# A gated hybrid-attention layer on one core: x enters the products without its norm, which is multiplied onto the products' columns

## The chip, the cores and the metric

The kernel runs on one core of one Trainium2 chip. The metric is the device time of one execution in microseconds (us); the time of a kernel is the median of several executions.

## The reference

One layer on x of 512 tokens (S) by 2048 features (D), everything in float32:

```
h    = x * rsqrt(mean(x*x) + eps) * norm_g
proj = h @ w_in                      # 3 branches x (q, k, v, gate) x 512, 4 forget logits, 3 x 2048 merge-gate logits
A: softmax attention with forget gates, q and k normalised per head     (4 heads of 128)
B: chunked attention with a relative bias, q and k normalised per head  (4 heads)
C: stick-breaking attention, q and k plain                              (4 heads)
y    = branch output * silu(gate);  up = y @ w_up (per branch)
out  = x + (sum over branches of sigmoid(merge gate) * up) @ w_out
```

The factor rsqrt(mean(x*x)+eps), called rstd below, is one number per token. norm_g is one number per feature.

## The kernel before, in words

All matrices are held transposed: a tile has 128 features on its partitions and the 512 tokens along its row. x is 16 such tiles, the k tiles (kt 0 to 15). A product of 128 output columns of w_in (a "column" below) with all of x is 16 k tiles of matmuls.

**Precision.** Each float32 operand is split in two fp32r parts: hi is a rounded copy made by ScalarE (L243), lo is the rest, made by VectorE (L247). A product takes hi*hi, hi*lo and lo*hi: three matmuls of 512 for each k tile. Weights come from HBM as raw tiles of 128x1024 (8 k tiles) and are split in the same way into `wh` and `wl`. There are three `wh` and three `wl` buffers, so the split runs two units ahead of TensorE (`LA = 2`). A unit is one weight tile with its matmuls.

**Two kinds of product.** A plain column (`col_task`, L554) is two units, 48 matmuls of 512. A `PairTask` (L603) makes two columns by a Strassen-like scheme over token halves and feature halves: seven units, each with 8 matmuls of 512 (one weight part times hi and lo of a half) and 8 of 256. It needs combinations of the raw weights (VectorE, L646 and L652, and one DMA that adds, issued by POOL in L278), combinations of x (`combos`, L506), and it folds its accumulators with VectorE and ScalarE (`after_of`, L697). The first pair is of a "late" form, which needs the combinations of x later.

**Order of the units.** `first_quad` (L1252) makes q, k, v and gate of head (C,0) at once, k tile after k tile as x arrives, and the forget logits: nine units, with kt 0, then 1, then two k tiles for each unit. Then come four plain merge-gate columns (`first_head`, L1333), the late pair, and eleven heads, each with a pair for q and k, a pair of merge gates, a pair for v and gate, and another pair of merge gates; head (C,1) has only one pair of merge gates. The attention of a head is cut into stages that are started at given units (`OFF`, L1640). Then `up_units` (L1420) and `out_pair` (L1540) follow.

**The norm.** Each k tile of x is multiplied by norm_g (`prep_x`, L426: VectorE L433 for kt below 10, ScalarE L436 above) and split; `first_quad` uses that unnormalised x. At the same time x is loaded a second time in natural layout (`xn`), squared and summed (L466), and `norm_x` (L460) makes rstd, spread over all partitions by one matmul (L481). `split_n` (L495) multiplies all 16 tiles by rstd (L501) and splits them again in place, and every later product uses the normalised x. The four columns of `first_quad` are multiplied by rstd when they are taken from PSUM (L1289), the forget logits too (L1300).

**What sets the order of instructions.** TensorE, ScalarE and VectorE run in a fixed order that a small planner (`Flow`, L63) writes down when the kernel is built: each task yields (engine, cost, due time), and on each engine the ready task with the earliest due time goes next. On the chip each engine takes its list strictly in order. SP issues nearly all loads and stores, POOL the adding DMAs. Work tiles of 128x512 come from a pool `t2` of 21 buffers (`NT`); raw weights have six.

Of the kernel before, what the change touches and what calls it, by code (L numbers as in the profile page):

```python
# [161 lines left out]
def hybrid_kernel(  # L162
# [126 lines left out]
    nc.scalar.dma_start(small_in, consts)  # L289
# [118 lines left out]
    norm_ev = [Event() for _ in range(KT)]  # L408
    used_q = [Event() for _ in range(KT)]
    used_g = [Event() for _ in range(UK)]  # L410
    x1 = [Parts("x1", [norm_ev[k], Event()]) for k in range(UK)]
    x2 = [Parts("x2", [norm_ev[k + UK]] * 2) for k in range(UK)]
# [6 lines left out]
    xps.free.clear()  # L419


    xnat = [xp.tile([P, 2, S], F32, tag="x", name=nm("xn")) for _ in range(UK)]
# [3 lines left out]
    def prep_x(kt):  # L426

        due = (5.0 + 3.2 * kt,)
        yield x_in[kt]
        x = xraw[kt]  # L430
        if kt < 10:
            yield (DVE, 0.5, *due)
            nc.vector.tensor_scalar_mul(x, x, gn[:, kt:kt + 1])  # L433
# [22 lines left out]

    rstd, rstd_ev = [], Event()
    n_split = [0]

    def norm_x():  # L460

        for i in range(NQ * QB):
            yield n_in[i]
            yield ACT, 0.75, 12.0 + 1.5 * i
            x = xnat[i // 2][:, i % 2, :]
            nc.scalar.activation(x, x, AF.Square, accum_out=ssq[:, i // NQ, i % NQ:i % NQ + 1])  # L466
        give(xps, UK)
        small_n = cp.tile([P, 5, QB], F32, name="small_n")
        y, m, tmp = small_n[:, 0, :], small_n[:, 1, :], [small_n[:, i, :] for i in range(2, 5)]
        yield DVE, 0.2  # L470
        nc.vector.tensor_reduce(m, ssq, axis=AX.X, op=ALU.add)
        yield from rsqrt(y, m, D, tmp, 4)
        yield t2s, 1
        dg = t2("dg")
        for b in range(QB):
            yield ACT, 0.3
            nc.scalar.activation(dg[:, blk(b)], identf, AF.Copy, scale=y[:, b:b + 1])
        yield atts, 1
        ps = att()
        yield PE, 0.9  # L480
        nc.tensor.matmul(ps, onef, dg, start=True, stop=True)  # L481
# [8 lines left out]
    def rstd_used():  # L490
        n_split[0] += 1
        if n_split[0] == KT + 5:
            give(t2s)

    def split_n(kt):  # L495

        due = (52.0 + 1.0 * kt + (8 if kt >= UK else 0),)
        yield raw_ev[kt]
        yield rstd_ev
        yield (DVE, dve_us(S), *due)  # L500
        nc.vector.tensor_mul(xraw[kt], xraw[kt], rstd[0])  # L501
        yield used_q[kt]
        yield from split(xs[kt].hi, xs[kt].lo, two(xraw[kt]), S, norm_ev[kt], due)
        rstd_used()

    def combos(k):  # L506

        due = (96.0 + k,)
        late = (106.0 + k,)
        a, b = xraw[k], xraw[k + UK]  # L510
        yield norm_ev[k]
        yield norm_ev[k + UK]
# [9 lines left out]
        yield used_g[k]  # L522
# [30 lines left out]

    def col_task(srcs, evac, bank=0, used=None):  # L554

        st = {}

        def mms(i):
            def go(u):
                if i == 0:  # L560
                    yield accs[bank], 1
                    st["ps"] = acc(bank)
                ps = two(st["ps"])
                for j in range(UK):
                    kt = i * UK + j
                    yield norm_ev[kt]
                    yield PE, mm_us(S, 2)
                    mm(ps, u.hi[:, j, :], xs[kt].hi, kt == 0)
                    mm(ps, u.hi[:, j, :], xs[kt].lo)
                yield u.ready  # L570
                for j in range(UK):
                    kt = i * UK + j
                    yield PE, mm_us(S)
                    mm(ps, u.lo[:, j, :], xs[kt].hi, stop=kt == KT - 1)
                    if used is not None and i == 0:
                        set_(used[j])
            return go

        def after():
            yield from evac(st["ps"])  # L580
            give(accs[bank])
        return [Unit(mms(i), after if i == 1 else None, srcs=[srcs[i]]) for i in range(2)]
# [336 lines left out]
    class Head:  # L919
# [53 lines left out]
        def plain(self, r):  # L973
            yield self.event(r)
            yield from self.turn()
            c = self.c[r]
# [111 lines left out]
        def stick_scores(self, j):  # L1088
            n = S - j * P
            for e in (("p", Q), ("p", K)):  # L1090
                yield self.event(*e)
            yield from self.room_of("z", j, 1)
# [9 lines left out]
            nc.scalar.activation(z, ps, AF.Copy, scale=SCALE)  # L1102
# [46 lines left out]
        def v_trans(self):  # L1149
# [10 lines left out]
            self.v = pair_of("v")  # L1160
            yield from split(*self.v, ps, S, self.event("v"))
            give(atts)

        def silu(self):

            yield self.event(G)
            g = self.c[G]
            yield t2s, 1
# [71 lines left out]
    def gate_units(late=False, x1_first=False):  # L1240
        n, d = gates.pop(0)

        def keep(i):
            def go(c):
                spill(n, d + i, c)
                return
                yield
            return go
        units.extend(PairTask(gate_col(n, d), gate_col(n, d + 1), ops, keep(0), None, keep(1), late,
                              x1_first=x1_first).units)  # L1250

    def first_quad(head):  # L1252

        c0 = head.n * 4 * NH + head.h
        ps = {}

        spans = [(0, 1), (1, 2)] + [(k, k + 2) for k in range(2, KT, 2)]

        def mms(i):
            def go(u):  # L1260
                if i == 0:
                    for r in (Q, K, V, G):
                        pool = atts if r in (V, G) else accs[0]
                        yield pool, 1
                        ps[r] = att() if r in (V, G) else acc()
# [18 lines left out]
        def take(r):  # L1284
            def go():
                yield t2s, 1
                yield DVE, dve_us(S)
                c = t2("c")
                nc.vector.tensor_mul(c, ps[r], rstd[0])  # L1289
                give(atts if r in (V, G) else accs[0])  # L1290
                rstd_used()
                head.c[r] = c
                set_(head.event(r))
            return go

        def take_f():
            yield t2s, 1
            yield DVE, dve_us(S)
            v = t2("f")[:2 * NH, :]
            nc.vector.tensor_mul(v, first_ps[:2 * NH, :], rstd[0][:2 * NH, :])  # L1300
            give(atts)
            rstd_used()
# [4 lines left out]
        def after():  # L1307
            for r in (Q, K, V, G):
                spawn(take(r)(), 1.0, flow.fin)
# [10 lines left out]
    def spilled(n, d):  # L1320
        def evac(ps):
            yield t2s, 1
            yield ACT, act_us(S)
            c = t2("c")
            nc.scalar.activation(c, ps, AF.Copy)
            spill(n, d, c)
        return evac

# [20 lines left out]
    def head(n, h, last=False):  # L1349
# [3 lines left out]
        if not last and (n, h) != (C, 1):  # L1353
# [3 lines left out]
        if last:  # L1357
            gate_units(x1_first=True)
# [225 lines left out]
    def loads():  # L1584
# [5 lines left out]
        def n(i):  # L1590
            n_in[i].t = fetch(xnat[i // 2][:, i % 2, :], xn[i // NQ, i % NQ], 0.0, 256).t

        order = [("x", 0), ("w", 0), ("x", 1), ("w", 1), ("x", 2), ("x", 3), ("w", 2)] + [("n", i) for i in range(6)]
        order += [("x", 4), ("x", 5), ("w", 3)] + [("n", i) for i in range(6, 12)] + [("x", 6), ("x", 7), ("w", 4)]
        order += [("n", i) for i in range(12, 16)] + [("x", 8), ("x", 9), ("w", 5)]
        order += [("x", i) for i in range(10, KT)]
        for kind, i in order:
            if kind == "x":
                yield from x(i)
            elif kind == "n":  # L1600
                n(i)
            else:
                yield from load_unit(units[i])
        for u in units[6:]:
# [20 lines left out]
    spawn(norm_x(), 5.0)  # L1625
    for kt in range(KT):
        spawn(split_n(kt), 5.0)
# [55 lines left out]
```

## Time and profile before

| what | value |
|---|---|
| time, median of 3 (lowest to highest) | 1346.86 us (1345.76 to 1347.42) |
| the profiled execution's own time | 1347.36 us |
| its span, first to last instruction | 1345.6 us |
| matmuls | 7514 |
| HBM read, written | 241.03 MB, 19.69 MB |

The profile is one execution. A page gives busy time by engine, a row of 40 slices of the span, a chain followed back from the last instruction, and groups of instructions. PE is TensorE's matmul queue, PEld its weight loads, DVE VectorE, ACT ScalarE. A row of a timeline is: start in us, how long, engine, line and operation, out<-in, shape, count, and in brackets the idle time ahead of it with what ended it. A matmul's shown time reaches beyond the start of the next one, since matmuls overlap; the step from start to start is what it costs.

### The profile page before, as it was taken

How to read it: one execution, taken by the hardware profiler on the slowest of the kernel's cores; microseconds unless marked ns; L12 is line 12 of the kernel's file. 1: busy time of each engine (PE TensorE's matmuls, PEld its weight loads, DVE VectorE, ACT ScalarE, POOL GpSimd, SP SyncE). 2: the span in 40 equal slices, each digit the busy share in tenths (PEclk: the TensorE clock that was granted, in tenths of full speed). 3: DMA queues.
4: the chain of work that ended last, by engine and by line, in shares of the span. 5: the costliest groups of instructions: out<-in, count | busy, mean ns of one | idle time of the engine just before them, and what ended most of it. 6: DMA issues, size and time to landing. Idle time of an engine off the chain costs nothing.

```text
span 1345.6 us, 20021 instructions
## 1 busy us (share of the span) xinstructions
PE 1333.1 (99%) x7514; PEld 1161.3 (86%) x7514; DVE 1098.2 (82%) x1585; ACT 801.3 (60%) x1240; POOL 94.2 (7%) x125
## 2 busy tenths in 40 slices
PE   7999999999999999999999999999999999999999
PEld 5789888888888888888888888888888888898888
DVE  5898997978878797787978878788788877797786
ACT  6656665656565666656666656656567655454543
POOL 0000000000001000010010101000000000000100
PEclk9999999999999999999999999999999999999999
DMA  9556666677677776776776777777767855658883
GB/s 305 197 145 170 161 169 191 164 211 190 179 193 200 193 191 191 192 198 194 188 200 183 187 195 178 191 189 201 180 173 222 288 201 189 200 148 246 252 243 102
DMA packets 91585, 262.03 MB, mean 195 GB/s; under 512 B 10184, under 2 KB 16968, under 8 KB 91488
## 3 DMA queue, kind: packets, MB, share of 16 engines
q1 hardware_dynamic: 72384, 201.69, 44.6%
q0 software_dynamic: 14976, 54.53, 24.5%
q10 hardware_dynamic: 4128, 4.53, 1.0%
q8 instruction: 59, 0.97, 0.3%
q14 instruction: 38, 0.31, 0.1%
HBM read 241.03 MB, written 19.69 MB: 194 GB/s over the span
## 4 chain that ended last, share of the span: by engine, by line
PE 95%; DMA 2%; DVE 1%; SPq 1%; issue 0%; ACT 0%; ACTq 0%; DVEq 0%
PE acc L262 82%; PE att L262 7%; DMA xn<-in_xn 1%; PE att L1130 1%; PE att L1059 1%; DMA raw<-in_w_col 1%; PE att L1197 1%; PE att L1198 1%; PE att L258 1%; PE att L259 1%; PE att L257 1%; PE att L1196 1%; DVE wl L247 1%; SPq L274 1%; PE att L1157 0%; DVE m L247 0%
## 5 line engine op out<-in xcount | busy, mean ns | idle before, releaser
L247 DVE TENSOR_TENSOR wl<-raw,wh 128x1024 fp32r<-128x1024 f32 (+2 forms) x413 | 493.8, 1196 | 161.9 <-ACT wh L243 161.4
L243 ACT ACTIVATE wh<-raw 128x1024 fp32r<-128x1024 f32 (+2 forms) x413 | 427.4, 1036 | 139.0 <-PE acc L262 59.8
L262 PE MATMUL acc<-x,wh 128*128 128x512 f32 (+1 forms) x1632 | 417.8, 391 | 7.4 <-ACT wh L243 7.4
L262 PEld LDWEIGHTS acc<-x,wh 128*128 128x128 f32 x1632 | 288.2, 189 | 58.1 <-ACT wh L243 8.1
L262 PE MATMUL acc<-t,wh 128*128 128x512 f32 (+1 forms) x1080 | 274.1, 390 | 0.0
L262 PEld LDWEIGHTS acc<-x,wl 128*128 128x128 f32 x1504 | 210.5, 190 | 19.0 <-DVE x L433 0.3
L262 PE MATMUL acc<-x,wl 128*128 128x256 f32 (+1 forms) x1504 | 223.6, 289 | 0.0
L262 PEld LDWEIGHTS acc<-t,wh 128*128 128x128 f32 x1080 | 189.5, 189 | 30.7
L262 PEld LDWEIGHTS acc<-t,wl 128*128 128x128 f32 x1056 | 144.8, 190 | 10.9
L262 PE MATMUL acc<-t,wl 128*128 128x256 f32 x1056 | 148.4, 282 | 0.0
L278 POOL DMA_DIRECT2D raw<-in_w_col x88 | 76.1, 865 | 939.2 <-DMA raw<-in_w_col 499.1
L262 PE MATMUL acc<-m,wh 128*128 128x512 f32 (+1 forms) x512 | 114.1, 366 | 0.3 <-DVE m L247 0.2
L262 PEld LDWEIGHTS acc<-m,wh 128*128 128x128 f32 x512 | 85.4, 189 | 13.6 <-DVE m L247 1.1
L830 ACT ACTIVATE c<-acc 128x256 f32<-128x256 f32 x49 | 18.8, 383 | 91.7 <-PE acc L262 88.7
L797 ACT ACTIVATE u<-acc 128x512 f32<-128x512 f32 x49 | 29.2, 596 | 73.1 <-PE acc L262 73.1
L262 PE MATMUL att<-y,wh 128*128 128x512 f32 x256 | 65.8, 389 | 0.0
L262 PEld LDWEIGHTS acc<-m,wl 128*128 128x128 f32 x448 | 60.5, 190 | 4.6 <-DVE wl L247 0.9
L646 DVE TENSOR_TENSOR raw<-raw,raw 128x1024 f32<-128x1024 f32 x52 | 63.4, 1219 | 0.5
L652 DVE TENSOR_TENSOR raw<-raw,raw 128x1024 f32<-128x1024 f32 x52 | 63.4, 1218 | 0.4
L262 PE MATMUL acc<-m,wl 128*128 128x256 f32 x448 | 62.6, 283 | 0.5 <-DVE wl L247 0.5
L780 ACT ACTIVATE v<-acc 128x512 f32<-128x512 f32 x50 | 29.9, 598 | 46.6 <-PE acc L262 46.6
L262 PEld LDWEIGHTS att<-y,wh 128*128 128x128 f32 x256 | 48.1, 188 | 9.9
(216 smaller groups left out, 1402.0 us busy)
## 6 DMA issues: line engine op xcount, KB each, us to landing
raw<-in_w_col SPq DMA_DIRECT2D x235, 512.0 KB, 4.4
raw<-in_w_col POOLq DMA_DIRECT2D x88, 512.0 KB, 6.4
raw<-in_w_out SPq DMA_DIRECT2D x40, 512.0 KB, 4.4
gl<-c SPq DMA_DIRECT2D x48, 256.0 KB, 2.4
raw<-in_w_up SPq DMA_DIRECT2D x32, 384.0 KB, 3.1
sg<-gl SPq DMA_DIRECT2D x48, 256.0 KB, 4.6
raw<-in_w_out POOLq DMA_DIRECT2D x16, 512.0 KB, 6.7
xn<-in_xn SPq DMA_DIRECT2D x16, 256.0 KB, 7.3
```

What stands on the lines that cost most here:

```text
L243: nc.scalar.activation(hi, src, AF.Copy)
L247: nc.vector.tensor_sub(lo, src, f(hi))
L257: nc.tensor.matmul(ps, lh, rh, start=start, stop=False, skip_group_check=more)
L258: nc.tensor.matmul(ps, lh, rl, start=False, stop=False, skip_group_check=more)
L259: nc.tensor.matmul(ps, ll, rh, start=False, stop=stop, skip_group_check=more)
L262: nc.tensor.matmul(ps, w, x, start=start, stop=stop, skip_group_check=more)
L278: nc.gpsimd.dma_start(to, src, accum_op=ALU.add)
L646: nc.vector.tensor_add(w[1], w[1], w[5])
L652: nc.vector.tensor_add(w[2], w[2], w[1])
L780: nc.scalar.activation(self.v, ps, AF.Copy)
L797: nc.scalar.activation(self.s, ps, AF.Copy)
L830: nc.scalar.activation(c, ps[:, RH], AF.Copy, scale=-1.0)
```

## The change

- `prep_x` splits x times norm_g straight from the loaded tile: ScalarE copies with the scale norm_g, VectorE computes x*norm_g - hi in one instruction. The tile itself is multiplied by norm_g later (kt even VectorE, odd ScalarE), for `combos`. x is never multiplied by rstd; `split_n` is gone.
- Every column that needs the norm is multiplied by the spread rstd when it is finished (`by_norm`): the 48 merge-gate columns, q and k of A and B, q of C, all gate columns, the forget logits. For C the keys' factor goes into the scale of the scores, and for all heads v gets it per token after its transposition, in four pieces of 128.
- The four plain merge-gate columns and `col_task` are gone. Their two pairs are made as pairs: one in head (C,1), one in the last head.
- `first_quad` takes its k tiles in the order 0, 1, 8-9, 2-3, 10-11, 4-5, 12-13, 6-7, 14-15, and q and k use other PSUM banks. Its columns are copied from PSUM without rstd.
- The loads: the second copy of x (`xn`) is loaded after the sixth unit's weights, three tiles for each unit, into `t2` buffers. The constants (norm_g among them) are loaded through POOL's queue instead of ScalarE's.
- `combos` is due earlier, and the stages of the first head start at other units.

The core of the diff:

```diff
-    nc.scalar.dma_start(small_in, consts)
+    nc.gpsimd.dma_start(small_in, consts)
...
     def prep_x(kt):
...
-        x = xraw[kt]
-        if kt < 10:
+        x, g, h, lo = xraw[kt], gn[:, kt:kt + 1], xs[kt].hi, xs[kt].lo
+        yield (ACT, act_us(S), *due)
+        nc.scalar.activation(h, two(x), AF.Copy, scale=g)
+        set_(raw_hi[kt])
+        yield (DVE, dve_us(S), *due)
+        nc.vector.scalar_tensor_tensor(lo, two(x), g, f(h), op0=ALU.mult, op1=ALU.subtract)
+        set_(raw_ev[kt])
+
+        due = (DUE[0] - 16.0 + place[kt],)
+        if kt % 2 == 0:
             yield (DVE, 0.5, *due)
-            nc.vector.tensor_scalar_mul(x, x, gn[:, kt:kt + 1])
+            nc.vector.tensor_scalar_mul(x, x, g)
         else:
             yield (ACT, 0.65, *due)
-            nc.scalar.activation(x, x, AF.Copy, scale=gn[:, kt:kt + 1])
-        yield from split(xs[kt].hi, xs[kt].lo, two(x), S, raw_ev[kt], due, raw_hi[kt])
+            nc.scalar.activation(x, x, AF.Copy, scale=g)
+        set_(gained[kt])
...
+    def by_norm(c, src=None):
+
+        yield rstd_ev
+        yield DVE, dve_us(S)
+        nc.vector.tensor_mul(c, c if src is None else src, rstd[0][:c.shape[0], :])
+        n_used[0] += 1
+        if n_used[0] == NB * DT + NB * NH + NH + 4 * NH + 1:
             give(t2s)
 
-    def split_n(kt):
-
-        due = (52.0 + 1.0 * kt + (8 if kt >= UK else 0),)
-        yield raw_ev[kt]
-        yield rstd_ev
-        yield (DVE, dve_us(S), *due)
-        nc.vector.tensor_mul(xraw[kt], xraw[kt], rstd[0])
-        yield used_q[kt]
-        yield from split(xs[kt].hi, xs[kt].lo, two(xraw[kt]), S, norm_ev[kt], due)
-        rstd_used()
...
         def keep(i):
             def go(c):
+                yield from by_norm(c)
                 spill(n, d + i, c)
...
-            yield from split(*self.v, ps, S, self.event("v"))
+            self.v = h, lo = pair_of("v")
+            yield rstd_ev
+            yield ACT, 4 * act_us(P)
+            for b in range(QB):
+                nc.scalar.activation(h[:, blk(b)], ps[:, blk(b)], AF.Copy, scale=rcol[:, b:b + 1])
+            yield DVE, 4 * dve_us(P)
+            for b in range(QB):
+                nc.vector.scalar_tensor_tensor(lo[:, blk(b)], ps[:, blk(b)], rcol[:, b:b + 1], f(h[:, blk(b)]),
+                                               op0=ALU.mult, op1=ALU.subtract)
...
-        cols = []
-        for _ in range(2):
-            g, d = gates.pop(0)
-            cols += [(g, d), (g, d + 1)]
-        t = [col_task(gate_col(*c), spilled(*c), b, used_g if i == 3 else None)
-             for i, (c, b) in enumerate(zip(cols, (1, 2, 0, 0)))]
-        for i in range(2):
-            units.extend(u[i] for u in t)
...
-        if not last and (n, h) != (C, 1):
+        if not last:
             gate_units()
...
         if last:
+            gate_units()
             gate_units(x1_first=True)
...
-OFF = dict(cs=3, ct=12, s=11, t=17, v=1, av=8, s1=8, t1=13, v1=0, av1=3, fb=31, a0=18, b0=28)
+OFF = dict(cs=3, ct=12, s=11, t=17, v=1, av=8, s1=8, t1=13, v1=0, av1=3, fb=24, a0=11, b0=20)
+
+DUE = 48.0, 58.0
+N_FROM, N_PER = 5, 3
```

More of the change, by code (lines that the diff above doesn't have):

```diff
@@ L418, in hybrid_kernel @@
     atts.free.pop()
-    xps.free.clear()
-    xnat = [xp.tile([P, 2, S], F32, tag="x", name=nm("xn")) for _ in range(UK)]
+    del xps.free[UK:]
+    spans = [(0, 1), (1, 2)] + [(k + h, k + h + 2) for k in range(0, UK, 2) for h in (0, UK)][1:]
+    place = {kt: i for i, kt in enumerate(kt for sp in spans for kt in range(*sp))}
     n_in = [Event() for _ in range(NQ * QB)]
@@ L552, in halves @@
         return [w_col[c, 0], w_col[c, 1]]
[L554 to L582, printed above, removed]
     class Pair(Unit):
@@ L974, in plain @@
             yield self.event(r)
+            c = self.c[r]
+            if r == Q:
+                yield from by_norm(c)
             yield from self.turn()
[L976 removed]
             yield t2s, 2
@@ L1167, in silu @@
             g = self.c[G]
+            yield from by_norm(g)
             yield t2s, 1
@@ L1284, in take @@
         def take(r):
-            def go():
-                yield t2s, 1
-                yield DVE, dve_us(S)
[L1288 to L1294, printed above, removed]
+            yield t2s, 1
+            c = t2("c")
+            if r in (Q, V):
+                yield ACT, act_us(S)
+                nc.scalar.activation(c, ps[r], AF.Copy)
+            else:
+                yield DVE, dve_us(S)
+                nc.vector.tensor_copy(c, ps[r])
+            give(pools[r])
+            head.c[r] = c
+            set_(head.event(r))
         def take_f():
+            yield rstd_ev
             yield t2s, 1
-            yield DVE, dve_us(S)
             v = t2("f")[:2 * NH, :]
-            nc.vector.tensor_mul(v, first_ps[:2 * NH, :], rstd[0][:2 * NH, :])
+            yield from by_norm(v, first_ps[:2 * NH, :])
             give(atts)
-            rstd_used()
             nc.sync.dma_start(fd, v)
@@ L1590, in n @@
         def n(i):
[L1591 to L1604, printed above, removed]
+            yield t2s, 1
+            t = t2("xn")
+            n_in[i].t = fetch(t, xn[i // NQ, i % NQ], 0.0, 256).t
+            spawn(square_x(i, t), 10.0)
+        todo = list(range(NQ * QB))
+        for i, sp in enumerate(spans):
+            for kt in [kt for sp in spans[i:i + 2 if i else 1] for kt in range(*sp)]:
+                if xraw[kt] is None:
+                    yield from x(kt)
+            yield from load_unit(units[i])
+            if i >= N_FROM:
+                for _ in range(N_PER):
+                    if todo:
+                        yield from n(todo.pop(0))
+        for i in todo:
+            yield from n(i)
+        for u in units[len(spans):]:
             yield from load_unit(u)
```

79 lines of the change are left out of this document (34 added, 45 removed).

## The prediction

> **What bounds the kernel now.** I read the page first, then what TensorE waited for, then the windows, then the timeline of the first 70 us.
>
> ```profile
> span 1345.6 us, 20021 instructions
> PE 1333.1 (99%) x7514; PEld 1161.3 (86%) x7514; DVE 1098.2 (82%) x1585; ACT 801.3 (60%) x1240; POOL 94.2 (7%) x125
> PE 95%; DMA 2%; DVE 1%; SPq 1%; issue 0%; ACT 0%; ACTq 0%; DVEq 0%
> ...
> PE acc L262 <- ACT wh L243: 7.4, 2, 7.0
> PE att L481 <- ACT dg L477: 1.2, 1, 1.2
> PE acc L262 <- DVE wl L247: 0.5, 1, 0.5
> PE acc L262 <- DVE m L247: 0.2, 1, 0.2
> ```
>
> TensorE is the bound. It is busy in 99% of the span, it is 95% of the chain that ended last, and it waited 9.3 us in all, of which 7.0 is its first start. So only two things can shorten the kernel by more than a few us: fewer matmul steps, or less standing still in the first stage.
>
> ```profile
> 0.00:20.00 20.00, 13.04 (x48) 9.57 (x49) 10.30 (x25) 10.25 (x22) 2.79 (x18) 1.00 0.86 292
> 20.00:40.00 20.00, 18.34 (x79) 13.09 (x77) 10.20 (x17) 16.67 (x41) 0.00 (x0) 1.00 1.01 333
> 40.00:60.00 20.00, 20.00 (x88) 15.01 (x87) 19.13 (x28) 14.85 (x23) 0.00 (x0) 1.00 0.56 194
> 60.00:80.00 20.00, 20.00 (x90) 16.33 (x89) 19.69 (x36) 8.05 (x11) 1.01 (x1) 1.00 0.52 130
> 120.00:1050.00 930.00, 930.00 (x5440) 820.41 (x5440) 767.54 (x1079) 582.97 (x898) 74.88 (x88) 1.00 0.72 190
> ```
>
> The columns are PE, PEld, DVE, ACT, POOL busy, then the granted clock, the DMA share and GB/s. In the first 40 us TensorE has holes while the DMA engines are full (share 0.86 and 1.01). From 40 us on it has none, and the clock is 1.00. From 120 to 1050 us VectorE works 767.5 of 930 us (83%) without holding TensorE up.
>
> **Part 1: two merge-gate pairs in place of four plain columns.**
>
> ```profile
> 63.61 3.79 PE L262 MATMUL acc<-x,wh 128*128 128x512 f32 x16
> 67.23 1.98 PE L262 MATMUL acc<-x,wl 128*128 128x512 f32 x8
> 69.05 3.79 PE L262 MATMUL acc<-x,wh 128*128 128x512 f32 x16
> ...
> 202.28 19.57 PE acc L262 x112
> ```
>
> A plain unit has 16 + 8 matmuls and takes 69.05 - 63.61 = 5.44 us. Four columns are eight units: 43.5 us. The last row is a stretch of seven pair units in the chain, 7 x (8 of 512 + 8 of 256) = 112 matmuls: 19.57 us for two columns. Two pairs take 39.1 us. TensorE is the bound at both places, so the gain is whole: **-4.4 us**. No other matmul is added or dropped; the attention has the same ones.
>
> **Part 2: the first stage.** The change takes 16 x 256 KB of `xn` out from between the first weights.
>
> ```profile
> 27.86 0.61 PE L262 MATMUL att<-x,wl 128*128 128x512 f32 x2
> 28.88 0.73 PE L262 MATMUL acc<-x,wh 128*128 128x512 f32 x2 [0.41 <-ACT wh L243]
> ...
> 37.65 0.40 PE L262 MATMUL att<-x,w 128*8 128x512 f32 x1
> 39.30 1.10 PE L481 MATMUL att<-dg,tmpc 128*128 128x512 f32 x2 [1.25 <-ACT dg L477]
> ```
>
> With 0.23 us from matmul to matmul, the two matmuls from 27.86 should be followed at 28.32, not 28.88: 0.56 us lost, to a weight split that waited for its DMA. The one at 37.65 should be followed at 37.88, not 39.30: 1.42 us lost, to the matmul that spreads rstd. Together 2.0 us. After the change a unit of 28 matmuls (some 6.5 us) needs 1 MB of x and weights, 160 GB/s, where the windows show 290 to 330: the first hole goes (-0.56). The matmul that spreads rstd stays, and in the changed kernel's order it comes after the sixth unit of `first_quad`'s nine, at about 47 us. What it waits for is late next: the last `xn` is issued behind a weight load whose buffer comes free with the fourth unit (about 36 us); with the 3 to 5 us that loads take it lands near 41, and behind it ScalarE has a weight split, a square, four half splits and the chain of small ones: I reach 46 to 47.5. Bounds: no wait (0) and the wait of before (1.42). I take **0.4**, so part 2 gives -0.56 - 1.42 + 0.4 = **-1.6 us**.
>
> **Part 3: the start.**
>
> ```profile
> 4.90 0.49 DVE L433 TENSOR_SCALAR x<-x,small_in 128x512 f32<-128x512 f32 x1 [0.20 <-DMA x<-in_xT]
> 5.42 0.63 ACT L243 ACTIVATE x<-x 128x512 fp32r<-128x512 f32 x1 [3.33 <-DVE x L433]
> 6.28 0.63 ACT L243 ACTIVATE wh<-raw 128x512 fp32r<-128x512 f32 x1 [0.23 <-DMA raw<-in_w_col]
> 6.96 0.80 PE L262 MATMUL acc<-x,wh 128*128 128x512 f32 x1 [6.96 <-ACT wh L243]
> ...
> small_in<-in_consts ACTq DMA_DIRECT2D x1, 66.5 KB, 3.2
> raw<-in_w_col POOLq DMA_DIRECT2D x88, 512.0 KB, 6.4
> ```
>
> VectorE's multiplication falls out of the first chain, and the first weights are issued first on ScalarE's queue. If the constants come in time, the x split can start at 4.90, the weight split 0.62 later, the first matmul 0.68 after that: 6.20, a gain of 0.76. But the split now needs the constants, which move to POOL's queue. Their old load took 3.2 us; POOL's loads took 6.4, with eight times the bytes and an addition. From an issue at 0.8 us that is 4.0 to 7.2, so the first matmul lies between 6.20 and 7.2 + 1.3 = 8.5: -0.8 to +1.5. The nearest row is the same load on the other queue; on SP the first x again has 256 KB ahead of it, now in smaller rows. I take **0**.
>
> By the Trainium skill, page "DMA: Bandwidth & Descriptors", section "Anatomy of one DMA — SWDGE (gpsimd) path", a load from POOL's queue takes about 2.0 us and its bytes at 436 GB/s, an estimate of 2.2 us here, so the constants would land before x, part 3 would be -0.8 instead of 0 and the sum 1340.1. No row of this trace shows a plain load on that queue.
>
> **Part 4: VectorE's and ScalarE's work.**
>
> ```profile
> L247 DVE TENSOR_TENSOR wl<-raw,wh 128x1024 fp32r<-128x1024 f32 x379 | 461.9, 1220 | 156.0 <-ACT wh L243 155.4
> L784 DVE TENSOR_TENSOR u<-u,acc 128x512 f32<-128x512 f32 x50 | 34.3, 686 | 13.2 <-PE acc L262 13.2
> L716 DVE TENSOR_TENSOR c<-u 128x256 f32<-128x256 f32 x99 | 42.0, 425 | 3.4
> L247 DVE TENSOR_TENSOR x<-x,x 128x512 fp32r<-128x512 f32 x32 | 21.1, 683 | 3.8 <-ACT x L243 3.8
> L501 DVE TENSOR_TENSOR x<-x,rstd 128x512 f32<-128x512 f32 x16 | 10.2, 679 | 0.0
> L1114 DVE TENSOR_TENSOR lk<-lk,m 128x128 f32<-128x128 f32 x16 | 4.7, 292 | 0.6
> ```
>
> Removed: 16 multiplications by rstd (10.2 us) and half of the 32 x splits (10.6). Added: 80 columns times rstd at 10.2/16 = 0.64 us, 51 us; four pieces of 0.29 for one of 0.68 in 12 heads, 6 us; for each new pair three more weight splits and two weight sums of 1.22 and about 3 x 0.69 + 4 x 0.42 of folding, 20 us for two. Net about +56 us, nearly all beside the heads: VectorE there goes from 83% to some 88%. I cost it at **0**, since TensorE's pair units hide it: the weight splits run two units (5.6 us) ahead, and VectorE's gaps of 162 us in that stretch are mostly waits for ScalarE's half of a weight split (155.4 us in the first row, over the span), not work that TensorE waits for. If that cover is gone, see rival 3. `by_norm` queues VectorE's list behind rstd only at the forget logits, some 13 us after rstd is there. Pulling `combos` and the second halves of x forward puts 8 x (4 + 4) x 0.42 = 27 us of VectorE into the first 60 us, where it now has 20 us idle and loses 16 second splits: summed in the changed order, it is through at about 60 us, and the late pair needs its first combination at about 64. The smaller moves (columns copied from PSUM by two engines, other PSUM banks, the scale in the scores) lie beside matmuls too: 0.
>
> **The sum.** -4.4 - 1.6 + 0 + 0 = -6.0 us. On the execution's own 1347.36 us (span 1345.6) that is 1341.4. The median of the runs, 1346.86, lies 0.5 lower: **1340.9 us**.
>
> **The rivals.**
>
> 1. *The first stage only swaps its holes.* The spread matmul waits as long as before, or the constants come late. For: TensorE and ScalarE meet within 1 us by my sum, and the chain for rstd has eight small steps across engines. Against: the DMA engines are no longer full. Price: with no gain in part 2 the pairs' 4.4 us alone are left, 1342.5; a late start adds up to 1.5, 1344.
>
> 2. *A new wait in each head.* q and k now pass `by_norm` first, and rstd holds one of 21 work buffers through all heads, so the scores of the B and A heads come later in TensorE's list and closer behind VectorE's splits of q and k. At one 0.7 us wait in each of eight heads: +5.6, 1346.5. Against: now TensorE waits for nothing there (0.5 us for a weight split in the whole span).
>
> 3. *VectorE becomes the bound* (the slower side).
>
> ```profile
> 150.00:160.00 10.00, 10.00 (x64) 8.90 (x64) 9.45 (x23) 8.46 (x16) 0.86 (x1) 1.00 0.62 156
> ...
> 510.00:520.00 10.00, 10.00 (x60) 8.86 (x59) 9.83 (x22) 5.60 (x12) 0.73 (x2) 1.00 0.53 127
> 520.00:530.00 10.00, 10.00 (x61) 8.76 (x60) 6.49 (x12) 6.96 (x12) 0.58 (x1) 1.00 0.71 210
> ...
> 980.00:990.00 10.00, 10.00 (x60) 8.87 (x59) 9.63 (x12) 5.11 (x8) 0.86 (x1) 1.00 0.55 141
> ```
>
> Of the 93 windows of 10 us from 120 to 1050, 24 show VectorE at 9.4 or more; the first and the last row here are the first and the last of them, the second is one more. If what is added there cannot move to a slacker window, 24/93 x 56 = 14 us come on top: 1355. It decides from the point where VectorE's backlog passes the two units, 5.6 us. Against: a full window is followed by a slack one (6.49 after 9.83), and 56 us over 93 windows is 0.6 us each.
>
> **How the numbers follow.** Forecast, 1338 to 1342.4: 0.50. Rival 1, 1342.4 to 1344.2: 0.20. Rival 2: 0.13, rival 3: 0.12. An earlier start than bounded here, below 1338: 0.05. The range 1338.0 to 1347.5 leaves out rival 3, the upper part of rival 2 and the tail below, some 0.2. A measurement tells about 0.2% (2.7 us) from no change: below 1344.2 lie the forecast, rival 1 and the tail, 0.74; within 0.2% most of rival 2, 0.14; above, rival 3, 0.12.
>
> **What would show it.** Right: some 7546 matmuls; no row of TensorE waiting for a weight split before 60 us; the first pair unit at about 61 us, right behind `first_quad`; VectorE 1150 us busy in all, 88% beside the heads, and still under 1 us of TensorE waiting for `wl`. Wrong: waits of TensorE for `qkl`, `lkl` or `p` in the heads (rival 2), for `wl` (rival 3), for `dg` over 1 us or a first matmul after 7.5 us (rival 1).

## The result, and the profile after

The changed kernel takes **1358.9 us** (median of 4 runs, 1358.6 to 1359.58), the kernel before, beside it, 1346.94: a ratio of 1.0091, 95% interval 1.0073 to 1.0108. It is 12 us slower, where 6 us faster was forecast, and outside the range. The span of the profiled execution is 1356.9 us, 11.3 more than before.

From the page of the changed kernel:

```profile
PE 1330.3 (98%) x7546; PEld 1161.4 (86%) x7546; DVE 1142.9 (84%) x1690; ACT 806.6 (59%) x1274; POOL 96.7 (7%) x130
PE 94%; DMA 4%; DVE 1%; ACT 1%; issue 0%; ACTq 0%; DVEq 0%
```

The chain that ended last has 4% of DMA instead of 2%. What TensorE waited for (engine, output tile and line, releaser: us in total, times, longest):

```profile
PE att L500 <- ACT dg L496: 12.3, 1, 12.3
...
PE acc L262 <- ACT wh L243: 9.9, 1, 9.9
```

Only two stops matter. One is the first start, at 9.94 us instead of 6.96. The other is new: the matmul that spreads rstd (L500) waits 12.3 us for `dg`. In the windows (columns as in the prediction: PE, PEld, DVE, ACT, POOL, clock, DMA share, GB/s) it is a hole in the first stage, and the clock falls with it:

```profile
40.00:50.00 10.00, 10.00 (x45) 7.53 (x44) 7.05 (x15) 6.70 (x16) 0.84 (x1) 1.00 0.88 278
50.00:60.00 10.00, 1.30 (x6) 0.75 (x4) 5.61 (x14) 4.97 (x15) 0.00 (x0) 0.82 0.61 160
60.00:70.00 10.00, 6.45 (x20) 4.26 (x21) 8.32 (x24) 8.59 (x27) 0.85 (x1) 0.67 0.45 105
```

TensorE's and ScalarE's timeline around the hole:

```profile
50.68 0.61 PE L262 MATMUL att<-x,wl 128*128 128x512 f32 x2
63.55 2.05 PE L500 MATMUL att<-dg,tmpc 128*128 128x512 f32 x2 [12.26 <-ACT dg L496]
64.61 1.84 PE L262 MATMUL acc<-x,wh 128*128 128x512 f32 x2
...
67.15 0.63 PE L262 MATMUL acc<-x,wh 128*128 128x512 f32 x2
```

```profile
51.37 0.71 ACT L447 ACTIVATE x<-x,small_in 128x512 f32<-128x512 f32 x1
57.11 0.63 ACT L478 ACTIVATE xn<-xn 128x512 f32<-128x512 f32 x1 [5.03 <-DMA xn<-in_xn]
...
57.73 1.04 ACT L243 ACTIVATE wh<-raw 128x1024 fp32r<-128x1024 f32 x1
58.68 0.61 ACT L478 ACTIVATE xn<-xn 128x512 f32<-128x512 f32 x1
...
62.14 1.26 ACT L496 ACTIVATE dg<-identf,small_n 128x128 f32<-128x128 f32 x4
```

Read them backwards: the matmul waits for `dg`; `dg` waits for the last squares; the last but one of these waits 5.03 us for its tile of `xn`, which lands at 57.1 us. After the stop, L500 and the next five matmuls take 67.15 - 63.55 = 3.60 us, where they take 2.09 in experiment 5, at a clock of 1.00 (49.71 to 51.80): another 1.5 us. From 120 us on there is nothing new: the row of the chain at which the `up` stage begins ("PE att L262 x24") starts at 1066.02, in the kernel before at 1055.30, 10.7 later; that at which the last stage begins ("PE acc L262 x752") at 1223.55 and 1212.77, 10.8 later.

The signed sum against before: start +3.0, the wait +12.3, the cold clock after it +1.5, the pairs -4.4, the two old holes -2.0: **+10.4** (the -4.4 as forecast, the rest read off the traces), against 10.7 measured at the `up` stage and 11.3 in the span; 0.5 of that is a later last landing.

### The profile page after: what moved, and what is told of

Read it like the earlier page. It is cut to its first block, busy times and chain, and to the rows that moved or that the text cites. A ratio compares the mean times of both kernels' runs of the same rounds, so it can differ in the third digit from the quotient of the medians.

```text
span 1356.9 us, 20287 instructions
## 1 busy us (share of the span) xinstructions
PE 1330.3 (98%) x7546; PEld 1161.4 (86%) x7546; DVE 1142.9 (84%) x1690; ACT 806.6 (59%) x1274; POOL 96.7 (7%) x130
## 4 chain that ended last, share of the span: by engine, by line
PE 94%; DMA 4%; DVE 1%; ACT 1%; issue 0%; ACTq 0%; DVEq 0%
PE acc L262 80%; PE att L262 7%; DMA xn<-in_xn 2%; DMA raw<-in_w_col 1%; PE att L1116 1%; PE att L1044 1%; PE att L257 1%; PE att L258 1%; PE att L1192 1%; PE att L1193 1%; PE att L259 1%; DMA x<-in_xT 1%; PE att L1191 1%; DVE wl L247 1%; PE att L1143 0%; DVE m L247 0%
## 5 line engine op out<-in xcount | busy, mean ns | idle before, releaser
L247 DVE TENSOR_TENSOR wl<-raw,wh 128x1024 fp32r<-128x1024 f32 (+2 forms) x419 | 500.5, 1197 | 149.9 <-ACT wh L243 143.1
L243 ACT ACTIVATE wh<-raw 128x1024 fp32r<-128x1024 f32 (+2 forms) x419 | 434.2, 1038 | 131.5 <-PE acc L262 65.6
L262 PE MATMUL acc<-x,wh 128*128 128x512 f32 (+1 forms) x1568 | 400.7, 391 | 9.9 <-ACT wh L243 9.9
L262 PEld LDWEIGHTS acc<-x,wh 128*128 128x128 f32 x1568 | 277.7, 190 | 59.9 <-ACT wh L243 9.9
L262 PE MATMUL acc<-t,wh 128*128 128x512 f32 (+1 forms) x1128 | 282.1, 389 | 0.0
L262 PEld LDWEIGHTS acc<-t,wh 128*128 128x128 f32 x1128 | 198.6, 189 | 33.3
L262 PEld LDWEIGHTS acc<-x,wl 128*128 128x128 f32 x1504 | 207.2, 190 | 16.7 <-DVE x L444 0.3
L262 PE MATMUL acc<-x,wl 128*128 128x256 f32 (+1 forms) x1504 | 216.5, 285 | 0.0
L262 PEld LDWEIGHTS acc<-t,wl 128*128 128x128 f32 x1104 | 151.8, 190 | 11.4
L262 PE MATMUL acc<-t,wl 128*128 128x256 f32 x1104 | 156.2, 282 | 0.0
L262 PE MATMUL acc<-m,wh 128*128 128x512 f32 (+1 forms) x512 | 114.1, 366 | 0.3 <-DVE m L247 0.2
L262 PEld LDWEIGHTS acc<-m,wh 128*128 128x128 f32 x512 | 85.4, 189 | 13.6 <-DVE m L247 1.1
L758 ACT ACTIVATE u<-acc 128x512 f32<-128x512 f32 x52 | 31.1, 599 | 75.3 <-PE acc L262 72.3
L779 ACT ACTIVATE u<-acc 128x512 f32<-128x512 f32 x51 | 30.3, 594 | 73.0 <-PE acc L262 72.9
L262 PE MATMUL att<-y,wh 128*128 128x512 f32 x256 | 65.8, 389 | 0.0
L262 PEld LDWEIGHTS acc<-m,wl 128*128 128x128 f32 x448 | 60.5, 190 | 4.6 <-DVE wl L247 0.9
L262 PE MATMUL acc<-m,wl 128*128 128x256 f32 x448 | 62.6, 283 | 0.5 <-DVE wl L247 0.5
L762 ACT ACTIVATE v<-acc 128x512 f32<-128x512 f32 x52 | 31.2, 600 | 43.9 <-PE acc L262 43.3
```

The lines of the kernel that those rows point to most:

```text
L243: nc.scalar.activation(hi, src, AF.Copy)
L247: nc.vector.tensor_sub(lo, src, f(hi))
L262: nc.tensor.matmul(ps, w, x, start=start, stop=stop, skip_group_check=more)
L758: nc.scalar.activation(self.u, ps, AF.Copy)
L762: nc.scalar.activation(self.v, ps, AF.Copy)
L779: nc.scalar.activation(self.s, ps, AF.Copy)
```

## The experiments

The theories. **A**: the loads set the end of the first stage; the matmul that spreads rstd stands too early in TensorE's fixed order for tiles of `xn` that land too late. **B**: the losses are separate and add up. **C**: the norm on the columns costs time in the heads, through VectorE. Later, under A, there was the question of *why* `xn` lands late: the bytes ahead of it in SP's queue, or the wait for a free buffer.

**1. The constants on ScalarE's queue again.**

```diff
-    nc.gpsimd.dma_start(small_in, consts)
+    nc.scalar.dma_start(small_in, consts)
```

> The changed kernel (1358.9 us) with one part undone: the constants go through ScalarE's queue again. Both theories expect the constants to land near 4 us and the first matmul near 6.5 us instead of 9.94. Theory A (the loads set the end of the first stage: the last xn lands at 57 us behind the weights, whatever TensorE does, and the matmul that spreads rstd waits for it): the matmul of the norm still starts at 62 to 64 us, TensorE's wait grows from 12.3 to about 15, and the time is 1357.5 to 1359. Theory B (the losses add up): the matmul of the norm moves forward with the start, and the time is 3 us shorter, 1355.9.

Measured: 1357.03 us, 1.0073 [1.0058, 1.0088] of before. The first matmul starts at 7.28 instead of 9.94, 2.66 earlier, but the wait for `dg` grows from 12.3 to 14.2:

```profile
PE att L500 <- ACT dg L496: 14.2, 1, 14.2
```

The time falls by 1.9 only: L500 starts at 61.54 instead of 63.55, since what it waits for comes only 2.0 earlier. That lies between the two theories: A had expected 1357.5 to 1359, B 1355.9. The late start was a cost, but a small part of it.

**2. The matmul that spreads rstd 109 matmuls later.** In `norm_x` a `yield norm_go` stands ahead of it, and the event is set with unit 11 (counted from 0), the third unit of the late pair. By the traces 277 matmuls stand ahead of it, 168 in the changed kernel; the 259 of the expectations count a late unit as 16 matmuls, and it has 24.

```diff
         at(OFF["fb"], forget_bias)
+        at(11, go_norm)
         gate_units(late=True)
```

> The changed kernel with one edit: the matmul that spreads rstd stands in TensorE's list inside the second late pair unit (after 259 matmuls) instead of after 168. Both theories: the wait of 12.3 us at that matmul and the cold clock behind it (about 1.5 us) go, 13.8 us in all, if nothing else is late next: 1345.1. Theory A: the split of the ninth unit's weights stands in ScalarE's list behind a square whose xn lands at 57 us, so TensorE waits 1 to 2 us for that split before the ninth unit: 1346 to 1347.

Measured: 1352.62 us, 1.0040 [1.0026, 1.0054], slower than either expectation. The wait for `dg` is gone, but three others take part of its place:

```profile
59.74 0.74 PE L262 MATMUL acc<-x,wh 128*128 128x512 f32 x2 [2.65 <-ACT wh L243]
68.41 3.60 PE L262 MATMUL acc<-x,wh 128*128 128x256 f32 x16 [1.94 <-ACT wh L243]
74.12 2.18 PE L262 MATMUL acc<-x,wh 128*128 128x256 f32 x16 [1.09 <-ACT c L1285]
```

They are ScalarE's: its list holds the squares too, and the first weight split stands behind a square that waits 5.08 us for `xn`; the two later ones come out of the work that has piled up by then, with ScalarE busy without a pause from 60 to 74 us. Moving the waiting matmul frees TensorE, not ScalarE.

**3. Both.**

> Both edits: constants on ScalarE's queue and the matmul that spreads rstd after 259 matmuls. Theory A: the start is 3 us earlier, but the ninth unit's weight split still waits for the xn that lands near 57 us, so TensorE gives the 3 us back there (a wait of 3 to 5 us): 1345 to 1347, as with the late matmul alone. Theory B: 1358.9 - 3.0 - 13.8 = 1342.

Measured: 1350.04 us, 1.0023 [1.0014, 1.0033], above A's 1345 to 1347 and far above B's 1342; the waits for weight splits stay (1.92 at 56.13, 1.96 at 64.79, and 1.09 at 70.51 for a copy). Two repairs take 8.9 of the 12 us, and the kernel is still behind.

**4. `xn` loaded earlier**: from the third unit on, six tiles a unit, in buffers of its own (`xp`, the pool from which the kernel before takes them), and the constants on ScalarE's queue; the matmul stays right behind the squares.

```diff
-            yield t2s, 1
-            t = t2("xn")
+            if i % 2 == 0:
+                yield xps, 1
+                xnat.append(xp.tile([P, 2, S], F32, tag="x", name=nm("xn")))
+            t = xnat[i // 2][:, i % 2, :]
...
-N_FROM, N_PER = 5, 3
+N_FROM, N_PER = 2, 6
```

> The changed kernel with its loads as before: the constants on ScalarE's queue, and xn loaded from the third unit on, six tiles for each unit, into its own buffers, so that the matmul that spreads rstd stands after 132 matmuls. Theory A: the last xn lands near 35 us, the first stage is that of the kernel before (waits of some 2 us, end near 63.5), and what is left of the change is the two pairs' 4.4 us: 1342.5, 1341 to 1344. Theory B gives the same. A third theory, that the norm on the products' columns itself costs time in the heads: 1347 or more.

Measured: **1344.34 us, 0.9977 [0.9968, 0.9986]**, faster than before. The last square is at 33.9 us. A hole of 1.29 us comes back at 31.11 (a weight split again), and `dg` is waited for 0.53. But this run changed three things: place, buffers and constants.

**5. Own buffers alone**: the buffer lines of the diff above, `N_FROM, N_PER` and the constants as in the changed kernel.

> The changed kernel, with the second copy of x loaded into the buffers that held raw x (its own ones), at the same place in the order of loads, so that no load waits for a square to free a work buffer; the matmul that spreads rstd comes after 169 matmuls instead of 168. If the loop from squares to loads holds the last xn back, the last square moves from 57 to about 48, TensorE's wait for dg falls from 12.3 to some 3 us, and the time from 1358.9 to about 1350. If it is the bytes ahead of xn in SP's queue, the last square stays at 55 or later, the wait above 10 us, and the time within 2 us of 1358.9.

Measured: **1343.41 us, 0.9973 [0.9964, 0.9983]**. The buffers alone take back 15.5 us, more than expected; 1.2 of it is the first matmul, at 8.78 instead of 9.94. The wait:

```profile
PE att L501 <- ACT dg L497: 0.8, 1, 0.8
```

SP's queue (start of the first issue of a row, how long the row took, count) shows why. The changed kernel:

```profile
34.24 3.96 SPq L274 DMA_DIRECT2D xn<-in_xn  x4
39.13 0.33 SPq L274 DMA_DIRECT2D raw<-in_w_col  x1
43.12 5.34 SPq L274 DMA_DIRECT2D xn<-in_xn  x4
48.79 0.33 SPq L274 DMA_DIRECT2D raw<-in_w_col  x1
49.52 0.98 SPq L274 DMA_DIRECT2D xn<-in_xn  x2
```

What its SP waited for in the first 66 us (releaser: us in total, times, longest); with own buffers there is no such row:

```profile
SPq L274 <- ACT xn L478: 9.0, 7, 3.3
```

Own buffers (the spread matmul stands behind 168 others, as in the changed kernel):

```profile
25.78 2.84 SPq L274 DMA_DIRECT2D xn<-in_xn  x4
28.72 0.59 SPq L274 DMA_DIRECT2D raw<-in_w_col  x1
30.83 2.96 SPq L274 DMA_DIRECT2D xn<-in_xn  x5
34.19 0.38 SPq L274 DMA_DIRECT2D raw<-in_w_col  x1
34.82 0.68 SPq L274 DMA_DIRECT2D xn<-in_xn  x1
```

The last issue is at 34.8 instead of 50.2, and SP no longer stands still between 39.5 and 43.1. The 16 raw tiles of x hold 16 of the 21 `t2` buffers; `xn` went round in those that were left, so a load waited for the square of an earlier tile. But SP's list changed too: of the late pair's five weights three stood ahead of the last ten `xn` and all five ahead of the last two, and now all five stand behind, presumably since nothing held `xn` up any more when the list was written. So buffer or bytes was still open.

**6. All three remedies without the earlier loads.**

> Own buffers for the second copy of x at the changed kernel's place in the order, constants on ScalarE's queue, and the matmul that spreads rstd after 259 matmuls instead of 168: all three remedies without the earlier loads. If ScalarE's list, held by squares that wait for xn, made the two waits of 1.9 us for weight splits that the two remedies without own buffers left (1350.0), they go, and the time is 1344 to 1346. If those waits come from the weights' own loads, standing behind as many bytes as before, they stay and the time is 1349 to 1350.

Measured: **1341.5 us, 0.9962 [0.9947, 0.9977]**, the fastest, and below both expectations. TensorE waits 7.4 us for its first start, and beside that 0.7 us in all for VectorE, as in the kernel before. The first pair unit of this version starts at 61.33, in the changed kernel at 78.86:

```profile
61.33 2.08 PE L262 MATMUL acc<-x,wh 128*128 128x256 f32 x16
```

Those 17.5 us close the account of the changed kernel: 9.94 - 7.37 = 2.6 from the start (from there to the end of the seventh unit, both take 41 us), 12.4 from the end of the seventh unit to L500, 1.1 for L500 itself, and 14.25 instead of 12.86 = 1.4 for the last two units, which begin on a cold clock. The times differ by 1358.9 - 1341.5 = 17.4.

**7. Bytes or buffer: own buffers, pair's weights ahead.** `PairTask.load` asks for four tiles of `xn` ahead of its fourth and of its fifth weight; SP's list should then have the pair's five weights ahead of the last two tiles, as in the changed kernel. By its rows it came out with four: SP issues 12 weights ahead of the last tile, 13 in the changed kernel, 8 with own buffers alone.

```diff
             for p, srcs in ((5, (a21, a22)), (1, (a11,)), (2, (a12,)), (7, (a11, a21)), (4, (a22,))):
+                if self is units[len(spans)].task:
+                    for _ in range({7: 4, 4: 4}.get(p, 0)):
+                        yield from more_n()
```

> With own buffers for the second copy of x, SP's list also changed: three weights of the late pair (1.5 MB) that stood ahead of the last ten tiles went behind them. Here the tiles have their own buffers, and the pair's weights are put back ahead: five of them (2.5 MB) stand before the last two tiles, as in the changed kernel. If the bytes ahead are the cause, 2 MB more at the 330 GB/s of this stage put the last square some 6 to 8 us later than with own buffers alone (44 us), at 50 to 52, and TensorE waits 6 to 8 us for dg: about 1350. If the wait for a free buffer is the cause, the last square stays within 3 us of 44, the wait below 3 us, and the time is 1343 to 1346.

Measured: 1342.97 us, 0.9971 [0.9961, 0.9981], but the run doesn't answer the question. The planner counts bytes, so it put the matmul behind 322 others by the trace (168 before; the 289 of the next expectation again counts a late unit as 16) and the squares up to 64.3 us. The time says nothing on it; only SP's queue does, with the last issue at 42.6.

**8. The same, with the bytes kept from the planner** (its load clock is set back after each of the pair's weights):

```diff
+                kept = line[:]
                 ev = fetch(t, srcs[0], flow.ready, 512)
...
+                if self is units[len(spans)].task and todo_n():
+                    line[:] = kept
```

> The run before on the same question left it open, since there the planner counted the bytes ahead and put the matmul that spreads rstd behind 289 matmuls. Here the second copy of x again has its own buffers and four weights of the late pair (2 MB) stand ahead of the last two tiles, but the planner does not count them: the squares stand early in ScalarE's list, and the matmul comes after 173 matmuls (168 in the changed kernel, own buffers alone 168). If the bytes ahead carry half of the delay (the last load was issued at 35 us with own buffers, 43 with the weights ahead, 50 in the changed kernel), the last square is near 50 and TensorE waits some 4 to 6 us for dg: 1347 to 1350. If the bytes are harmless and only the wait for a free buffer counts, the wait is below 1.5 us and the time 1343 to 1344.5; if the bytes are all of it, the wait is 10 us or more and the time above 1353.

Measured: 1348.31 us, 1.0010 [1.0000, 1.0019]. TensorE's timeline and the windows:

```profile
54.44 1.22 PE L501 MATMUL att<-dg,tmpc 128*128 128x512 f32 x2 [3.04 <-ACT dg L497]
54.97 1.54 PE L262 MATMUL acc<-x,wh 128*128 128x512 f32 x2
```

```profile
54.00:55.00 1.00, 0.56 (x3) 0.36 (x3) 0.81 (x4) 1.00 (x4) 0.52 (x1) 1.00 0.67 111
55.00:56.00 1.00, 1.00 (x4) 0.58 (x3) 0.51 (x3) 1.00 (x2) 0.33 (x1) 0.64 1.02 201
56.00:57.00 1.00, 1.00 (x4) 0.68 (x3) 1.00 (x1) 1.00 (x4) 0.00 (x0) 0.50 1.20 205
57.00:58.00 1.00, 1.00 (x3) 0.66 (x2) 1.00 (x3) 1.00 (x4) 0.00 (x0) 0.50 1.01 193
58.00:59.00 1.00, 1.00 (x4) 0.73 (x3) 1.00 (x3) 1.00 (x5) 0.00 (x0) 0.66 1.01 201
59.00:60.00 1.00, 1.00 (x6) 0.80 (x5) 1.00 (x4) 0.40 (x2) 0.00 (x0) 1.00 0.39 74
```

The last square, with own buffers alone and here (in the changed kernel it is at 58.7):

```profile
43.91 0.61 ACT L478 ACTIVATE xn<-xn 128x512 f32<-128x512 f32 x1
50.16 0.63 ACT L478 ACTIVATE xn<-xn 128x512 f32<-128x512 f32 x1
```

So of the delay of 14.8 us, 6.3 come with the weights that this run puts ahead, and 8.5 are left for the wait for a buffer. That is a bound on each, not a measurement: SP issues 11 weights ahead of the last tile here, so three of the pair's five are back, not four as the expectation says. At 6.3 / 3 = 2.1 us for each, an estimate, all five would carry 10.5 and the buffers 4.3. That the buffers count as well is seen in SP's own queue: 9.0 us behind squares in the changed kernel, no such row here or in experiment 5. A clean split is not shown, and there may be none, since a square that frees a buffer waits for a load itself.

Of TensorE's wait (0.8, 3.0, 12.3) the weights carry 2.3 here and the rest is 9.2. The first 6.3 us show as 2.3 only because `dg` starts 2.87 us after the last square instead of 4.39, and because TensorE comes to the spread matmul 2.4 later, with five more matmuls ahead of it (1.1) and 1.3 behind already at the unit before. The run is 1348.31 - 1343.41 = 4.9 us slower than own buffers alone; at the first pair unit (68.68 and 63.51) it is 5.2, of which 2.3 are the wait, 1.6 the cold clock and 1.3 what TensorE was behind already.

**9. Every column multiplied by rstd twice** (on top of experiment 4).

```diff
         nc.vector.tensor_mul(c, c if src is None else src, rstd[0][:c.shape[0], :])
+        yield DVE, dve_us(S)
+        nc.vector.tensor_mul(c, c, rstd[0][:c.shape[0], :])
```

> The version with early xn loads and constants on ScalarE's queue (1344.3), in which every column that needs the norm is multiplied by rstd twice: the output is not the reference's, and VectorE has some 81 x 0.66 = 53 us more work, nearly all beside the heads, 84% to 88% of the span. If VectorE's work lies hidden beside TensorE's pairs, the time rises by less than 2 us: 1344 to 1346. If the heads were at VectorE's bound in the windows where it is busy above 94%, a quarter of it shows: +14, 1358; if it sets the heads altogether, +50.

Measured: 1346.75 us (1344.41 to 1350.14), against 1344.34 for experiment 4. From 120 to 1050 us:

```profile
120.00:1050.00 930.00, 928.95 (x5403) 818.38 (x5402) 844.04 (x1234) 582.37 (x915) 74.90 (x88) 1.00 0.73 192
```

VectorE is busy for 844 of 930 us (91%), 39 us more than in experiment 4 (804.7), and TensorE stands still for 1.05. Theory C falls: the heads hide the multiplication of each column, and nearly all of a second one. At 91% the cover begins to thin: 1.05 us shows in the trace, 2.4 between the medians, a little more than the 2 expected. The trace is of an execution of 1344.89 us; what made others take up to 1350.14 it cannot show.

**10. The kernel before, with its constants on POOL's queue.**

> The kernel before with one line changed: the constants are loaded through POOL's queue. If this load is late by itself (it took 7.3 us in the changed kernel and 3.2 on ScalarE's queue), the first matmul starts near 9.5 to 10 us instead of 6.96, VectorE's first multiplication waits for small_in, and the time is 2 to 3 us above the kernel before: 1349 to 1350. If the load is late only because of what else the changed kernel does at its start (ScalarE's queue carries the first weights there), it lands near 4 to 5 us here and the time stays within 1 us.

Measured: 1347.53 us, 1.0002 [0.9993, 1.0012]. Each expectation was half right: the load takes 5.2 us there and the first matmul starts at 9.04, 2.1 later than before, yet the time is the same. Both holes of the old first stage are gone instead. This fits a stage whose end the loads set: TensorE started late only to stand still less. So theory B fails there: the start and the holes behind it are one quantity, not two. Where no load sets the end, a start does count: from experiment 5 to 6 the first matmul moves from 8.78 to 7.37, 0.8 us of waiting for `dg` go, and the time falls by 1.9.

**11. The load by itself.** The probe computes nothing of the layer; it ran once.

```diff
+    for name, queue in (("pool_a", nc.gpsimd), ("act_a", nc.scalar), ("pool_b", nc.gpsimd), ("act_b", nc.scalar)):
+        last[0] = load(name, queue)
...
+    busy("pool_c", nc.gpsimd, 6)
+    busy("act_c", nc.scalar, 6)
+    busy("pool_d", nc.gpsimd, 6)
+    busy("act_d", nc.scalar, 6)
```

> A probe that computes nothing of the layer and stores zeros: the 66.5 KB of constants are loaded four times alone, one load after the other (POOL's, ScalarE's, POOL's, ScalarE's queue), and four times beside six loads of 256 KB on SP's queue, again alternating. If POOL's queue is slow by itself, its loads alone take 5 us or more where ScalarE's take about 2.5. If its load loses against other loads in flight, the two queues agree alone (2 to 3 us), and beside the six loads POOL's takes 5 us or more where ScalarE's takes 3 to 4. If neither shows, the first use of POOL's queue in the execution is what costs, and only the first of its loads is slow.

Measured (us from issue to landing at the end of each row; a and b alone, c and d beside six loads of 256 KB on SP's queue):

```profile
pool_a<-in_consts POOLq DMA_DIRECT2D x1, 66.5 KB, 2.2
act_a<-in_consts ACTq DMA_DIRECT2D x1, 66.5 KB, 1.9
pool_b<-in_consts POOLq DMA_DIRECT2D x1, 66.5 KB, 2.1
act_b<-in_consts ACTq DMA_DIRECT2D x1, 66.5 KB, 1.8
pool_c<-in_consts POOLq DMA_DIRECT2D x1, 66.5 KB, 3.0
act_c<-in_consts ACTq DMA_DIRECT2D x1, 66.5 KB, 2.6
pool_d<-in_consts POOLq DMA_DIRECT2D x1, 66.5 KB, 3.9
act_d<-in_consts ACTq DMA_DIRECT2D x1, 66.5 KB, 2.6
```

Alone, the two queues nearly agree, and the first use is not slower than the second. Beside other loads POOL's loses more, but 3.9 us is short of the 7.3 in the changed kernel. So POOL's load misses the 5 us or more that the second explanation asked for. That the rest comes from the denser traffic at a kernel's start is argued, not shown.

## Why the prediction was wrong

- **Part 1, right.** The matmuls are 7546; a stretch of 112 pair matmuls still takes 19.57 us, and the heads have no new stop. The sum of the result closes within 0.3 us with the -4.4 in it; no run measures them alone.
- **Part 2 is the step that failed**, at the sentence that the last `xn` "lands near 41". I followed one issue, "behind a weight load whose buffer comes free with the fourth unit", and asked neither which buffers the `xn` tiles themselves would get nor what SP's order puts ahead of them. The last issue is at 50.2 instead of 36, and the last two tiles are squared from 57.1 and 58.7. The kernels have the answer: before, `xn` has eight double buffers of `xp` for itself; after, it is `t2("xn")`, 21 buffers, 16 held by x. Experiments 5 and 8 show both causes, the buffers and the pair's weights ahead; of the 14.8 us between them at least 6.3 come with the weights and at most 8.5 with the buffers. In the changed kernel the term measured 12.3 instead of 0.4, and 1.5 for the clock, which I had not priced at all.
- In the same sentence "the 3 to 5 us that loads take" was too short by the page of the kernel before, whose row for these very loads has 7.3 (median, issue to landing):

```profile
xn<-in_xn SPq DMA_DIRECT2D x16, 256.0 KB, 7.3
```

- The prediction places the spread matmul after the sixth unit. The 168 matmuls ahead of it are seven units (2 x 14 + 5 x 28); the "about 47 us" is the time of seven.
- With own buffers the last square is at 43.9, the wait for `dg` is 0.8 where I had 0.4, and the time is 1343.41; with an earlier start and a later spread matmul too it is 1341.5, against 1340.9. So the other terms hold in a kernel without that loop, though these two are not the kernel that was predicted.
- "The DMA engines are no longer full" failed with it: their share from 10 to 40 us is 0.96 to 1.05, since the loads that the change takes from the start are queued into the same 60 us.
- **Part 3, wrong in size.** The term of 0, with bounds of -0.8 and +1.5, measured +3.0: the constants came 7.3 us after their issue at 1.34, at 8.65, where my upper end was 7.2. VectorE's and ScalarE's first rows:

```profile
8.65 0.17 DVE L340 COPY gq<-small_in 128x4 f32<-128x4 f32 x1 [4.97 <-DMA small_in<-in_consts]
8.65 0.72 ACT L435 ACTIVATE x<-x,small_in 128x512 fp32r<-128x512 f32 x1 [6.56 <-DMA small_in<-in_consts]
```

- The estimate of 2.2 us for this load, worked out from the Trainium skill's page "DMA: Bandwidth & Descriptors", section "Anatomy of one DMA — SWDGE (gpsimd) path", is what experiment 11 measures for the load alone (2.2 and 2.1). The kernel's start is not that case.
- **Part 4, right.** VectorE is busy for 1142.9 us (1150 forecast; 44.7 more than before, where 56 were summed), for 803.8 of 930 us beside the heads (86%; 88% forecast), and TensorE waits 0.5 us for `wl`, as before. Rivals 2 and 3 did not happen; experiment 9 shows how far off the third was.
- **Rival 1** had the right place, the spread matmul and late constants, and the wrong price: 1344 at most, because I bounded the wait by that of before (1.42). A wait that hangs on loads has no such bound. The slower side was given to VectorE, and 0.12.

## What to carry to other kernels

When a change moves loads, look up the pool that each moved tile is taken from, count what else holds that pool at that time, and follow the in-order queue behind the tile: a load that waits for a buffer stops the queue, and whatever is ready may be put ahead of it. A stop of a strictly ordered engine is bounded by when the data can come, not by how long the same wait was before. If loads set the end of a stage, a late start and the holes after it are one sum; if they don't, the start counts by itself.

## What the runs showed of the hardware

- **The clock falls after short stops too, depending on when they come.** In experiment 8 a stop of 3.0 us left the granted clock at 1.00 while it lasted; then it was 0.50 to 0.66 from 55 to 59 us, with TensorE already at work. In experiment 3 two stops of 1.9 us behaved differently: around the one that ends at 56.13 the clock stays 1.00, after that at 64.79 it is 0.50. Nor does the longer stop decide: in experiment 2 one of 2.65 us (to 59.74) left the clock at 1.00, and one of 1.94 (to 68.41) was followed by 0.50. The rows of experiment 3, then of 2:

```profile
56.00:58.00 2.00, 1.87 (x8) 1.47 (x9) 1.89 (x4) 2.00 (x8) 0.00 (x0) 1.00 0.03 8
...
64.00:66.00 2.00, 1.21 (x9) 1.21 (x10) 1.74 (x4) 2.00 (x6) 0.00 (x0) 0.96 0.95 190
66.00:68.00 2.00, 2.00 (x12) 2.00 (x11) 2.00 (x4) 2.00 (x5) 0.00 (x0) 0.50 0.16 29
```

```profile
60.00:62.00 2.00, 2.00 (x10) 1.38 (x10) 2.00 (x5) 2.00 (x9) 0.00 (x0) 1.00 0.03 8
...
70.00:72.00 2.00, 2.00 (x11) 2.00 (x10) 2.00 (x4) 2.00 (x6) 0.00 (x0) 0.50 0.00 0
```

- The Trainium skill, page "TensorE: Matmul & The Clock Gate", section "Part 1: The HAM clock gate (the "warmup" mystery)", tells of a window of 3.4 us that runs freely and of half the clock after an idle one. The half clock of experiment 8 fits that length (from 55 to 59 us, (0.36 + 0.50 + 0.50 + 0.34) / 0.5 = 3.4 us), and that a longer stop can pass where a shorter one does not fits a window that runs freely; but stops of 1.9 and 3.0 us, shorter than the window, were enough.
- **A load on POOL's queue takes longer beside other loads**: 66.5 KB took 2.2 us alone, 3.0 and 3.9 beside six loads, and 5.2 to 7.4 at the start of six kernels; on ScalarE's queue 1.9 alone, 2.6 beside six loads, and 3.2 to 3.3 at the start of three.
